# Ordering the casts of the middle features behind the weights' casts, and the loads for the weight sums behind other loads

## The chip, the core and the metric

One NeuronCore of a Trainium2 chip runs the whole layer as one program. The metric is the device time of one execution in microseconds (us). The kernel before takes 2896.6 us, the median of 3 runs (2887.7 to 2897.81).

## What is computed

The reference is one decoder layer on 2048 tokens of width 1024. The change touches its last line alone, the feed-forward part:

```python
h = rmsnorm(x, norm_mlp[l]) * (1.0 + sc_m) + sh_m
x = x + g_m * (jnp.square(jax.nn.relu(h @ w_ff1[l])) @ w_ff2[l])
```

`w_ff1` is 1024 x 4096 and `w_ff2` is 4096 x 1024, all in float32.

## The kernel before, in words

**Precision.** TensorE multiplies numbers of type float32r. Every float32 operand is therefore split into a high part, which is a cast to float32r on ScalarE, and a low part, which is the operand minus the high part. A product needs three matmuls: high by high, high by low, low by high. The weights' parts are `swh` and `swl` (function `left`, L1137 to L1144): the cast at L1142 on ScalarE, the subtraction at L1143 on VectorE in the first layer and on GpSimd in the second.

**Seven products for eight.** Both layers use a fast 2 x 2 block scheme: seven block products of sums of blocks, taken in the order `ORDER` = 0, 4, 5, 2, 6, 3, 1, instead of eight. The sums of `w_ff1` blocks (s4, s5, s2, s6) are made on GpSimd while the kernel runs (`lefts1`, L1146). The sums of `w_ff2` blocks are made once by `sums2` (L1233): it loads two tiles of 512 KB (L1238), makes four sums (L1239 and L1241 on GpSimd, L1240 and L1242 on VectorE) and stores two tiles to DRAM as `w2_d` (L1244).

**The loops.** The tokens are worked in two halves, `hf` = 1 and then 0. In each, the first layer runs 16 groups `g` of 256 middle features (`ff1`), seven products of 12 matmuls each, and stores the seven right-hand operands of each group to DRAM as `h_d` (256 KB each). In the first half only, each group also calls `sums2(g)`. Then the second layer (`ff2`) runs twice (`q` = 0, 1), 56 blocks each: 7 products by 8 groups. A block loads 256 KB of weights into `w` (L1323, 4 buffers, tag S), 256 KB of middle features into `bl` (L1325), casts them into `bh` (L1326, ScalarE), subtracts (L1327, VectorE), splits the weights (L1142, L1143) and does 12 matmuls (L1332 to L1334). `bh` and `bl` have 28 buffers each, `swh` and `swl` three. `load_y` fetches the tiles that the results are added to, and in the first half `load_h` prepares the next half's features; the scheduler places their instructions among those of the first layer's end and of `ff2`.

**What sets the order.** A scheduler writes each engine's instructions down in one fixed order when the kernel is built, and an engine works through its own list in that order. An instruction that waits holds up all behind it on that engine. Almost all loads and stores are issued by SyncE (SP), whose list is in order too. `tc.issue_after(x)` adds no semaphore; it makes the scheduler place what stands in the block behind `x` on the same engine. `gate["w1"]` is the latest load of `w_ff1` blocks (L1153).

Of the kernel before, what the change touches and what calls it, by code (L numbers as in the profile page):

```python
# [7 lines left out]
F32 = mybir.dt.float32  # L8
# [49 lines left out]
def tile_hybrid_layer(  # L58
# [17 lines left out]
    nc = tc.nc  # L76
    V, G, A, T = nc.vector, nc.gpsimd, nc.scalar, nc.tensor
# [56 lines left out]
    if True:  # L134
        def sb(name, bufs=1, stack=mx, side="left"):
            return stack.enter_context(tc.tile_pool(name=name, bufs=bufs, side=side))
# [9 lines left out]
        at = sb("at", 1, right, "right")  # L146
# [18 lines left out]
        gate = {"dma": None, "pe": None}  # L165
# [88 lines left out]
        def rstd(accs, which, name, pool=None, tag="mm"):  # L254


            v, r, t = [cp.tile([P, 4], F32, tag=n + which, name=n + name) for n in ("nv", "nr", "nt")]
            dg = accs[0]

            def sums():  # L260
                st = (pool or pm).tile([P, 4], F32, tag=tag, name="ss" + name)
                with tc.issue_after(gate["pe"]) if gate["pe"] is not None else nullcontext():
                    for b in range(4):
                        for i, acc in enumerate(accs):
                            T.matmul(st[:, b:b + 1], lhsT=acc[:, b * P:(b + 1) * P], rhs=ones[:, 0:1], start=i == 0,
                                     stop=i == len(accs) - 1)
                with tc.high_priority():
                  V.tensor_scalar(v, st, 1.0 / D, EPS, ALU.mult, ALU.add)
                  rsqrt(r, v, t)
                  for b in range(4):  # L270
                    V.tensor_scalar(dg[:, b * P:(b + 1) * P], ident, r[:, b:b + 1], None, ALU.mult)

            def spread():
                ps = (pool or pm).tile([P, CH], F32, tag=tag, name="rsp" + name)
                T.matmul(ps, lhsT=ones, rhs=dg, start=True, stop=True)
                A.copy(dg, ps)
            return sums, spread
# [748 lines left out]
        for k, tag in enumerate(("mt1", "mt0", "bv1", "bv0", "kw1", "kw0", "AT1", "AT0")):  # L1026
            x = dn.tile([P, CH], F32, tag=tag, name=f"x0_{k}")
# [56 lines left out]
        ORDER = (0, 4, 5, 2, 6, 3, 1)  # L1084
        fb = right.enter_context(tc.tile_pool(name="fb", bufs=28, side="right", reuse_waits="tile"))

        def right_tile(name):

            return [fb.tile([P, CH], F32R, tag=f"b{i}", name=f"b{i}{name}") for i in "hl"]
# [44 lines left out]

        def left(x, name, eng):  # L1137

            wh = wp.tile([P, CH], F32R, tag="wh", name="swh" + name)
            wl = wp.tile([P, CH], F32R, tag="wl", name="swl" + name)  # L1140
            with tc.high_priority():
                A.copy(wh, x)  # L1142
                eng.tensor_tensor(wl, x, wh.bitcast(F32), SUB)  # L1143
            return wh, wl  # L1144

        def lefts1(hf, g, unit):  # L1146

            nm = f"{hf}_{g}"
            a = []
            with tc.high_priority():  # L1150
                for i, t in enumerate(AB):
                    u = unit(t, f"{t}_1{nm}")
                    gate["w1"] = nc.sync.dma_start(u, w_ff1[g, i]).ins  # L1153
                    a.append(u)
                a11, a12, a21, a22 = a
                s4, s5, s2, s6 = [unit("S", f"s{i}{nm}") for i in (4, 5, 2, 6)]
                G.tensor_tensor(s4, a21, a22, ADD)
                G.tensor_tensor(s5, s4, a11, SUB)
                G.tensor_tensor(s2, a12, s5, SUB)
                G.tensor_tensor(s6, a11, a21, SUB)  # L1160
            xs = (a11, a12, s2, a22, s4, s5, s6)
            return lambda j: left(xs[j], f"{nm}_{j}", V)
# [27 lines left out]
        def unit(tag, name):  # L1190
            return fu.tile([P, CH], F32, tag=tag, name=name)
# [31 lines left out]
        def load_y(hf):  # L1223
            ys = []
            for k in range(KT):
                y = fy.tile([P, N2], F32, tag="y", name=f"y{hf}_{k}")
                for i in range(2):
                    with tc.issue_after(gate["w1"]):
                        nc.sync.dma_start(y[:, i * CH:(i + 1) * CH], x1_d[2 * hf + i][:, k, :])
                ys.append(y)  # L1230
            return ys

        def sums2(g):  # L1233

            y = [fy.tile([P, N2], F32, tag="y", name=f"ws2_{g}_{i}") for i in range(3)]
            (a11, a12), (a21, a22), (s4, s5) = [(t[:, 0:CH], t[:, CH:N2]) for t in y]
            for i in range(2):
                nc.sync.dma_start(y[i].rearrange("p (i c) -> p i c", i=2), w_ff2[g, 2 * i:2 * i + 2].rearrange("i p c -> p i c"))  # L1238
            G.tensor_tensor(s4, a21, a22, ADD)  # L1239
            V.tensor_tensor(s5, s4, a11, SUB)  # L1240
            G.tensor_tensor(a11, a11, a21, SUB)  # L1241
            V.tensor_tensor(a12, a12, s5, SUB)  # L1242
            for i in range(2):
                nc.sync.dma_start(w2_d[g][:, 2 * i:2 * i + 2], y[2 - 2 * i].rearrange("p (i c) -> p i c", i=2))  # L1244
# [56 lines left out]
            G.tensor_tensor(t4, t2, t21, SUB)  # L1301
            put(3, t4)

        def ff2(hf, q, ys):


            n1, n2 = 0, CH
            dst = {0: ((0, n1),), 1: ((0, n1),), 5: ((0, n2),), 2: ((0, n2),), 4: ((4, n2),), 6: ((4, n1), (4, n2)),
                   3: ((4, n1),)}
            chain = {0: "u", 5: "u", 6: "u", 4: "v", 2: "v", 3: "p", 1: "q"}  # L1310
            a, banks = q % 2, {}
            side = {"u": a, "v": 1 - a, "p": 1 - a, "q": a}
            final = {n: j for j in ORDER for n in dst[j]}
            for j in ORDER:
                ch = chain[j]
                start = ch not in banks
                if start:
                    banks[ch] = [pf.tile([P, CH], F32, tag=f"f{side[ch]}", name=f"f2{hf}_{q}_{j}{m}") for m in range(4)]
                for i in range(8):
                    g = 8 * q + i  # L1320
                    nm = f"2{hf}_{g}_{j}"
                    x, bt = unit("S", "w" + nm), right_tile(nm)
                    nc.sync.dma_start(x, {0: w_ff2[g, 0], 1: w_ff2[g, 1], 3: w_ff2[g, 3]}[j] if j in (0, 1, 3) else  # L1323
                                      w2_d[g][:, {4: 0, 5: 1, 6: 2, 2: 3}[j], :])
                    nc.sync.dma_start(bt[1].bitcast(F32), h_d[hf][g][:, j, :])  # L1325
                    A.copy(bt[0], bt[1].bitcast(F32))  # L1326
                    V.tensor_tensor(bt[1], bt[1].bitcast(F32), bt[0].bitcast(F32), SUB)  # L1327
                    wh, wl = left(x, nm, G)
                    for m in range(4):
                        s = slice(m * P, (m + 1) * P)  # L1330
                        ps = banks[ch][m]
                        T.matmul(ps, lhsT=wh[:, s], rhs=bt[0], start=start and i == 0, stop=False, skip_group_check=True)  # L1332
                        T.matmul(ps, lhsT=wh[:, s], rhs=bt[1], start=False, stop=False, skip_group_check=True)  # L1333
                        T.matmul(ps, lhsT=wl[:, s], rhs=bt[0], start=False, stop=i == 7, skip_group_check=True)  # L1334
                with tc.high_priority():
                    for m in range(4):
                        for m0, cs in dst[j]:
                            y = ys[m0 + m][:, cs:cs + CH]
                            gt = ngate[:, m0 + m:m0 + m + 1] if j == 3 else mods[:, 40 + m0 + m:41 + m0 + m]
                            V.scalar_tensor_tensor(y, banks[ch][m], gt, y, ALU.mult, ALU.add)  # L1340
                            if q == 1 and final[m0, cs] == j:
                                nc.sync.dma_start(yTv[:, m0 + m, hf * N2 + cs:hf * N2 + cs + CH], y)
# [6 lines left out]
        for hf in (1, 0):  # L1349
            if not hf:  # L1350
                get = lefts1(0, 0, unit)
            for g in range(NG):
                more = lefts1(hf, g + 1, unit) if g + 1 < NG else None
                if hf:
                    sums2(g)
                ff1(hf, g, bs, get)
                get = more
                if hf and g == 1:
                    for f in rstd([accs2[0]], "2", "20", pf, "f0"):
                        f()  # L1360
                if not hf and g == 4:
                    ys = load_y(0)
            if hf:
                ys = load_y(1)
            for q in range(2):
                ff2(hf, q, ys)
            if hf:
                bs = load_h(0, [accs2[0], accs2[1]])

# [87 lines left out]
```

## Time and profile before

| what | value |
|---|---|
| median of 3 runs | 2896.6 us |
| the profiled execution | 2896.35 us |
| its span, first to last instruction | 2894.6 us |
| TensorE busy (PE) | 2603.6 us, 90% |
| first layer, first half | 1537 to 1875 us of the span |
| second layer, first half | 1875 to 2242 us |
| first layer, second half | 2242 to 2547 us |
| second layer, second half | 2547 to 2891 us |

PE is TensorE's matmuls and PEld its weight loads, DVE is VectorE, ACT ScalarE, POOL GpSimd, SP SyncE. Matmuls are pipelined, so that a matmul's own time counts the one behind it too: read PE's speed by counting matmuls in a stretch, not by busy time. In a table of windows "(xN)" is the number of instructions that fall into the window, and PEclk is the share of the full TensorE clock that was granted.

### The profile page before, as it was taken

The page shows a single profiled execution, that of the slowest core. Times are in us where ns is not written, and L with a number is a line of the kernel's source. Part 1 is how long each engine was busy: PE and PEld are TensorE (multiplying, and loading weights), DVE is VectorE, ACT ScalarE, POOL GpSimd, SP SyncE. Part 2 cuts the span into 40 slices and gives each one's busy share as a digit, 9 for nine tenths or more (in the row PEclk, how much of TensorE's full clock was granted, in tenths as well). Part 3 has the DMA queues.
Part 4 walks back from the last instruction along what each step waited for, and adds up shares of the span by engine and source line. Part 5 has one row for each costly group of instructions (what it writes and reads, how often), then busy time and mean ns, then how long its engine had stood idle before and what let it go on. Part 6 is the DMA issues. An engine that isn't in the chain of part 4 may idle for free.

```text
span 2894.6 us, 40750 instructions
## 1 busy us (share of the span) xinstructions
PE 2603.6 (90%) x13684; PEld 2086.0 (72%) x13684; DVE 1575.3 (54%) x3359; ACT 1288.6 (45%) x2622; POOL 1049.7 (36%) x837
## 2 busy tenths in 40 slices
PE   4898799999989999888397999989999999999999
PEld 3687578877888688766275778866767888876667
DVE  7654886376437773375636664663335544473321
ACT  4553453346324553254432555653333555563331
POOL 3222201030103101131336786444448565553434
PEclk9999889999989999898698999999999999999999
DMA  8786677565556546352367974765544454485554
GB/s 306 267 286 208 225 270 250 169 209 168 179 171 201 184 155 215 122 183 82 100 201 268 319 255 148 271 236 160 168 152 146 155 206 149 147 282 161 167 156 135
DMA packets 327315, 566.86 MB, mean 196 GB/s; under 512 B 33512, under 2 KB 80552, under 8 KB 327080
## 3 DMA queue, kind: packets, MB, share of 16 engines
q1 hardware_dynamic: 308904, 534.63, 56.0%
q10 hardware_dynamic: 18176, 29.37, 2.8%
q8 instruction: 114, 1.87, 0.3%
q14 instruction: 121, 0.99, 0.1%
HBM read 403.86 MB, written 160.01 MB: 195 GB/s over the span
## 4 chain that ended last, share of the span: by engine, by line
PE 30%; issue 9%; POOL 9%; DMA 3%; DVE 2%; ACT 1%; POOLq 0%; SPq 0%; DVEq 0%; ACTq 0%
POOL swl L1143 6%; PE f L1257 6%; PE f L1259 6%; PE f L1258 6%; PE f L1334 3%; PE f L1333 3%; PE f L1332 3%; DMA bl<-h_d 1%; PE mmo L221 1%; PE mmo L222 1%; PE mmo L223 1%; DMA fx<-x_d 1%; POOL fx L1205 0%; POOL ws L1239 0%; DMA A<-in_w_ff_dram 0%
## 5 line engine op out<-in xcount | busy, mean ns | idle before, releaser
L1143 POOL TENSOR_TENSOR swl<-w,swh 128x512 fp32r<-128x512 f32 x224 | 304.8, 1363 | 379.5 <-ACT swh L1142 332.8
L1334 PE MATMUL f<-bh,swl 128*128 128x512 f32 x896 | 346.8, 405 | 32.8 <-POOL swl L1143 32.1
L1332 PE MATMUL f<-bh,swh 128*128 128x512 f32 x896 | 357.8, 399 | 19.5 <-ACT swh L1142 19.0
L1257 PE MATMUL f<-bh,swh 128*128 128x512 f32 x896 | 352.4, 393 | 16.3 <-ACT swh L1142 12.8
L1327 DVE TENSOR_TENSOR bl<-bl,bh 128x512 fp32r<-128x512 f32 x224 | 183.8, 836 | 333.8 <-ACT bh L1326 333.5
L1259 PE MATMUL f<-bh,swl 128*128 128x512 f32 x896 | 347.4, 393 | 12.6 <-DVE swl L1143 12.6
L1333 PE MATMUL f<-bl,swh 128*128 128x512 f32 x896 | 352.9, 394 | 0.0
L1258 PE MATMUL f<-bl,swh 128*128 128x512 f32 x896 | 351.1, 392 | 0.0
L1326 ACT CAST bh<-bl 128x512 fp32r<-128x512 f32 x224 | 136.8, 621 | 322.0 <-DMA bl<-h_d 287.2
L1334 PEld LDWEIGHTS f<-bh,swl 128*128 128x128 f32 x896 | 168.9, 189 | 107.7 <-POOL swl L1143 75.2
L1332 PEld LDWEIGHTS f<-bh,swh 128*128 128x128 f32 x896 | 169.9, 190 | 73.4 <-ACT swh L1142 38.3
L1257 PEld LDWEIGHTS f<-bh,swh 128*128 128x128 f32 x896 | 169.9, 190 | 54.9 <-ACT swh L1142 13.6
L1259 PEld LDWEIGHTS f<-bh,swl 128*128 128x128 f32 x896 | 169.5, 189 | 51.6 <-DVE swl L1143 16.4
L1258 PEld LDWEIGHTS f<-bl,swh 128*128 128x128 f32 x896 | 169.8, 189 | 35.2
L1333 PEld LDWEIGHTS f<-bl,swh 128*128 128x128 f32 x896 | 170.4, 190 | 30.7
L1143 DVE TENSOR_TENSOR swl<-s,swh 128x512 fp32r<-128x512 f32 x126 | 139.2, 1108 | 97.3 <-ACT swh L1142 97.0
L1142 ACT CAST swh<-w 128x512 fp32r<-128x512 f32 x224 | 138.2, 619 | 89.8 <-PE f L1333 67.0
L221 PE MATMUL mmo<-hm,who 128*128 128x512 f32 x256 | 103.4, 411 | 45.3 <-ACT hm L950 45.3
L932 POOL TENSOR_TENSOR o<-o,ro 128x512 f32<-128x512 f32 x16 | 16.7, 1042 | 323.7 <-DVE ro L129 159.3
L1143 DVE TENSOR_TENSOR swl<-A,swh 128x512 fp32r<-128x512 f32 x95 | 88.2, 928 | 77.3 <-ACT swh L1142 77.2
L1270 DVE TENSOR_TENSOR t<-t,f 128x512 f32<-128x512 f32 x128 | 87.1, 683 | 76.5 <-PE f L1259 73.3
L1271 ACT ACTIVATE t<-t 128x512 f32<-128x512 f32 x128 | 80.7, 630 | 86.6 <-DVE t L1270 86.6
(380 smaller groups left out, 6108.3 us busy)
## 6 DMA issues: line engine op xcount, KB each, us to landing
bl<-h_d SPq DMA_DIRECT2D x224, 256.0 KB
A<-in_w_ff_dram SPq DMA_DIRECT2D x128, 256.0 KB
h_d<-t SPq DMA_DIRECT2D x128, 256.0 KB
w<-w_d SPq DMA_DIRECT2D x128, 256.0 KB
wada<-in_w_ada_dram SPq DMA_DIRECT2D x48, 512.0 KB
h_d<-T SPq DMA_DIRECT2D x96, 256.0 KB
w<-in_w_ff_dram SPq DMA_DIRECT2D x96, 256.0 KB
wso<-in_w_out_dram SPq DMA_DIRECT2D x64, 256.0 KB
```

The costliest lines, as they stand in the source:

```text
L221: T.matmul(ps, lhsT=wh[:, k % 4, :], rhs=ah, start=k == 0, stop=False)
L1142: A.copy(wh, x)
L1143: eng.tensor_tensor(wl, x, wh.bitcast(F32), SUB)
L1257: T.matmul(ps, lhsT=wh[:, s], rhs=ah, start=start and k == 0, stop=False, skip_group_check=True)
L1258: T.matmul(ps, lhsT=wh[:, s], rhs=al, start=False, stop=False, skip_group_check=True)
L1259: T.matmul(ps, lhsT=wl[:, s], rhs=ah, start=False, stop=stop and k == 3, skip_group_check=True)
L1270: V.tensor_tensor(t, t, ps, op)
L1326: A.copy(bt[0], bt[1].bitcast(F32))
L1327: V.tensor_tensor(bt[1], bt[1].bitcast(F32), bt[0].bitcast(F32), SUB)
L1332: T.matmul(ps, lhsT=wh[:, s], rhs=bt[0], start=start and i == 0, stop=False, skip_group_check=True)
L1333: T.matmul(ps, lhsT=wh[:, s], rhs=bt[1], start=False, stop=False, skip_group_check=True)
L1334: T.matmul(ps, lhsT=wl[:, s], rhs=bt[0], start=False, stop=i == 7, skip_group_check=True)
```

## The change

Three edits. `left` now notes every weights' cast in a list, `casts`. The cast of the middle features of block `at` of a second layer is placed behind the weights' cast of block `at - 22` (for the first 25 blocks behind one of a nearer block, down to three casts before the layer begins). The two loads of `sums2` are placed behind the latest load of `w_ff1` blocks.

```diff
+        casts = []
+
         def left(x, name, eng):
...
             with tc.high_priority():
-                A.copy(wh, x)
+                casts.append(A.copy(wh, x).ins)
                 eng.tensor_tensor(wl, x, wh.bitcast(F32), SUB)
...
             for i in range(2):
-                nc.sync.dma_start(y[i].rearrange("p (i c) -> p i c", i=2), w_ff2[g, 2 * i:2 * i + 2].rearrange("i p c -> p i c"))
+                with tc.issue_after(gate["w1"]):
+                    nc.sync.dma_start(y[i].rearrange("p (i c) -> p i c", i=2), w_ff2[g, 2 * i:2 * i + 2].rearrange("i p c -> p i c"))
...
-        def ff2(hf, q, ys):
+        def ff2(hf, q, ys, base):
...
-            for j in ORDER:
+            for n, j in enumerate(ORDER):
...
-                    A.copy(bt[0], bt[1].bitcast(F32))
+                    at = 56 * q + 8 * n + i
+                    with tc.issue_after(casts[base + max(at - 22, at // 4 - 3)]):
+                        A.copy(bt[0], bt[1].bitcast(F32))
...
+            base = len(casts)
             for q in range(2):
-                ff2(hf, q, ys)
+                ff2(hf, q, ys, base)
```

The change adds and removes no instruction; it moves some. Three places follow. A name ends in the tile's numbers: `bh21_4_1` belongs to the second layer (2), half 1, group 4, product 1; `A11_11_0` is block A11 of the first layer's half 1, group 0.

ScalarE in the second layer, first half, `q` = 0, product 2 (blocks 28 to 31 are groups 4 to 7 of product 2), first before and then with the change. Product 1 is the last of the seven, so group 4 of it is block 52 and group 2 of it block 50.

```order
L1326 CAST bh21_4_1_32501<-bl21_4_1_32502 128x512
L1142 CAST swh21_4_2_31931<-w21_4_2_31924 128x512
L1326 CAST bh21_5_1_32524<-bl21_5_1_32525 128x512
L1142 CAST swh21_5_2_31954<-w21_5_2_31947 128x512
L1326 CAST bh21_6_1_32547<-bl21_6_1_32548 128x512
L1142 CAST swh21_6_2_31977<-w21_6_2_31970 128x512
```

```order
L1331 CAST bh21_2_1_32455<-bl21_2_1_32456 128x512
L1144 CAST swh21_5_2_31954<-w21_5_2_31947 128x512
L1331 CAST bh21_3_1_32478<-bl21_3_1_32479 128x512
L1144 CAST swh21_6_2_31977<-w21_6_2_31970 128x512
L1331 CAST bh21_4_1_32501<-bl21_4_1_32502 128x512
L1144 CAST swh21_7_2_32000<-w21_7_2_31993 128x512
```

Before, the features' cast of block 52 stands right ahead of the weights' cast of block 28, so 25 blocks ahead of the last weights' cast (27); with the change it stands behind the weights' cast of block 30, 22 ahead. SP's order of loads in this stage does not change: each weights' load of block m is followed by the features' load of block m + 22.

SP at the start of the first layer's first half, first before and then with the change; `fw_0` and the `A` tiles are blocks of `w_ff1`, `ws2` the loads of `sums2`, `w2_d` its stores.

```order
L1238 DMA ws2_0_0_28421<-in_w_ff2_dram 128x2x512
L1238 DMA ws2_0_1_28422<-in_w_ff2_dram 128x2x512
L1174 DMA fw_0_28349<-in_w_ff1_dram 128x512
L1238 DMA ws2_1_0_28586<-in_w_ff2_dram 128x2x512
L1238 DMA ws2_1_1_28587<-in_w_ff2_dram 128x2x512
L1244 DMA w2_d0_28333<-ws2_0_2_28423 128x1024
L1244 DMA w2_d0_28333<-ws2_0_0_28421 128x1024
L1238 DMA ws2_2_0_28790<-in_w_ff2_dram 128x2x512
L1153 DMA A11_11_0_28389<-in_w_ff1_dram 128x512
```

```order
L1176 DMA fw_0_28349<-in_w_ff1_dram 128x512
L1155 DMA A11_11_0_28389<-in_w_ff1_dram 128x512
L1155 DMA A11_11_1_28405<-in_w_ff1_dram 128x512
L1155 DMA A12_11_0_28391<-in_w_ff1_dram 128x512
L1155 DMA A12_11_1_28407<-in_w_ff1_dram 128x512
L1155 DMA A21_11_0_28393<-in_w_ff1_dram 128x512
L1155 DMA A21_11_1_28409<-in_w_ff1_dram 128x512
L1155 DMA A22_11_0_28395<-in_w_ff1_dram 128x512
L1155 DMA A22_11_1_28411<-in_w_ff1_dram 128x512
L1241 DMA ws2_0_0_28421<-in_w_ff2_dram 128x2x512
```

The nine loads of `w_ff1` blocks now go first. From there on one pair of `ws2` loads follows per group up to the last, where before all 16 pairs stood within the first seven groups.

POOL and DVE in the first layer's first half around groups 8 and 9, with the change; before, the same rows stand in the same order without the four of `ws2_9`.

```order
L1302 TENSOR_TENSOR T1_7_1_29823<-t1_7_3_29689,T1_7_0_29822 128x512
L1162 TENSOR_TENSOR s61_9_29847<-A11_11_9_29836,A21_11_9_29840 128x512
L1304 TENSOR_TENSOR T1_7_2_29824<-T1_7_1_29823,t1_7_2_29688 128x512
L1242 TENSOR_TENSOR ws2_9_2_30031<-ws2_9_1_30030 128x512
L1244 TENSOR_TENSOR ws2_9_0_30029<-ws2_9_0_30029,ws2_9_1_30030 128x512
L1159 TENSOR_TENSOR s41_10_30021<-A21_11_10_30017,A22_11_10_30019 128x512
```

```order
L1145 TENSOR_TENSOR swl1_9_0_30045<-A11_11_9_29836,swh1_9_0_30044 128x512
L1273 TENSOR_TENSOR t1_8_3_29866<-t1_8_3_29866,f11_8_0_29871 128x512
L1243 TENSOR_TENSOR ws2_9_2_30031<-ws2_9_2_30031,ws2_9_0_30029 128x512
L1273 TENSOR_TENSOR t1_8_2_29865<-t1_8_2_29865,f11_8_3_29963 128x512
L1245 TENSOR_TENSOR ws2_9_0_30029<-ws2_9_0_30029,ws2_9_2_30031 128x512
L1145 TENSOR_TENSOR swl1_9_4_30063<-s41_9_29844,swh1_9_4_30062 128x512
```

The low part for product 4 of group 9 now stands behind two sums of `sums2(9)` on DVE, and the sum s4 of group 10 behind two on POOL.

## Rows read from the trace of the kernel before

**Rows 1.** The page's first part: busy time, share, instructions of the engines.

```profile
PE 2603.6 (90%) x13684; PEld 2086.0 (72%) x13684; DVE 1575.3 (54%) x3359; ACT 1288.6 (45%) x2622; POOL 1049.7 (36%) x837
```

**Rows 2.** Windows, one per second layer: length, engines' busy time, PEclk, DMA share, GB/s.

```profile
1875.00:2242.00 367.00, 333.03 (x1348) 249.79 (x1348) 165.59 (x209) 150.51 (x262) 183.90 (x133) 0.98 0.55 177
2547.00:2891.00 344.00, 324.68 (x1346) 248.04 (x1344) 129.96 (x168) 122.91 (x216) 154.33 (x114) 1.00 0.53 171
```

**Rows 3.** Windows of L1334 alone (4 matmuls a block): PE, PEld, PEclk, DMA, GB/s.

```profile
1936.00:2173.00 237.00, 119.55 (x292) 54.82 (x291) 0.99 0.51 158
...
2604.00:2827.00 223.00, 113.00 (x276) 52.21 (x276) 0.99 0.51 161
2827.00:2889.00 62.00, 35.42 (x92) 17.15 (x92) 1.00 0.40 127
```

**Rows 4.** Windows of L1259 alone (first layer, 4 matmuls a product).

```profile
1537.00:1702.00 165.00, 79.00 (x196) 38.09 (x196) 0.95 0.88 313
...
1855.00:1875.00 20.00, 10.29 (x27) 5.07 (x27) 1.00 0.99 356
2242.00:2527.00 285.00, 160.56 (x419) 78.75 (x420) 1.00 0.46 161
```

**Rows 5.** Waits from 1936 to 2173: us in total, times, longest us.

```profile
ACT bh L1326 <- DMA bl<-h_d: 140.1, 67, 4.1
POOL swl L1143 <- ACT swh L1142: 109.8, 59, 4.0
...
PEld f L1334 <- POOL swl L1143: 33.8, 51, 1.4
```

**Rows 6.** Timelines of POOL, SP and ACT, 2041 to 2056: start, us, what [idle before].

```profile
2042.40 1.30 POOL L1143 TENSOR_TENSOR swl<-w,swh 128x512 fp32r<-128x512 f32 x1 [0.70 <-ACT swh L1142]
...
2043.73 0.33 SPq L1323 DMA_DIRECT2D w<-in_w_ff_dram  x1
2044.16 0.37 SPq L1325 DMA_DIRECT2D bl<-h_d  x1
...
2047.15 0.62 ACT L1326 CAST bh<-bl 128x512 fp32r<-128x512 f32 x1 [0.85 <-DMA bl<-h_d]
2047.67 0.62 ACT L1142 CAST swh<-w 128x512 fp32r<-128x512 f32 x1
...
2048.37 1.30 POOL L1143 TENSOR_TENSOR swl<-w,swh 128x512 fp32r<-128x512 f32 x1 [0.70 <-ACT swh L1142]
```

**Rows 7.** Timelines of SP, ACT and POOL where the first layer begins, 1529 to 1548.

```profile
1529.96 0.90 SPq L1238 DMA_DIRECT2D ws<-in_w_ff_dram  x2
1533.12 0.34 SPq L1174 DMA_DIRECT2D fw<-in_w_ff_dram  x1
...
1541.06 5.54 SPq L1153 DMA_DIRECT2D A<-in_w_ff_dram  x9
...
1536.69 1.14 ACT L1142 CAST swh<-fw 128x512 fp32r<-128x512 f32 x2 [4.94 <-DMA fw<-in_w_ff_dram]
...
1535.38 1.26 POOL L1239 TENSOR_TENSOR ws<-ws 128x512 f32<-128x512 f32 x1 [2.29 <-DMA ws<-in_w_ff_dram]
```

**Rows 8.** Timelines of POOL, SP and DVE in one group without sums, 1757 to 1780.

```profile
1758.20 1.30 POOL L1157 TENSOR_TENSOR s<-A,A 128x512 f32<-128x512 f32 x1 [5.92 <-DVE swl L1143]
...
1766.63 1.75 POOL L1299 TENSOR_TENSOR T<-t,T 128x512 f32<-128x512 f32 x1
...
1770.00 0.33 SPq L1153 DMA_DIRECT2D A<-in_w_ff_dram  x1
...
1776.47 0.69 DVE L1143 TENSOR_TENSOR swl<-s,swh 128x512 fp32r<-128x512 f32 x1
```

**Rows 9.** Groups of DVE from 1537 to 1702: xcount, busy us, mean ns, idle.

```profile
L1143 DVE TENSOR_TENSOR swl<-A,swh 128x512 fp32r<-128x512 f32 x21 | 25.3, 1204 | 8.2 <-ACT swh L1142 8.2
```

**Rows 10.** Windows of all engines where the second layer's first half begins.

```profile
1850.00:1860.00 10.00, 10.00 (x46) 8.29 (x45) 6.11 (x7) 6.20 (x12) 4.09 (x4) 1.00 0.50 146
1860.00:1900.00 40.00, 30.91 (x133) 24.28 (x131) 36.22 (x42) 29.54 (x54) 19.12 (x13) 0.94 1.05 401
```

## The prediction

> **What bounds the kernel now.** I read the page's busy times first, then windows over the four feed-forward stages, then the waits and timelines inside them. TensorE is busy for 90% of the span [rows 1], so only time in which TensorE is held up can be won. The windows of the two second layers [rows 2] show stages of 367 and 344 us in which no other engine is busy for more than half the time and DMA has a share of 0.55: nothing is full, so something waits in turn.
>
> How fast could TensorE go there? Count matmuls. In the first layer of the second half, 419 matmuls of L1259 stand in 285 us [rows 4]; four make a product of twelve, so a product takes 285 / 104.75 = 2.72 us, at a granted clock of 1.00. The end of the last second layer shows that its blocks of twelve can do the same: 92 matmuls of L1334, 23 blocks, in 62 us, 2.70 us each [rows 3]. From block 88 or so there are no features' casts left in ScalarE's list. Ahead of that, 73 blocks took 237 us in the first half and 69 blocks 223 us in the second [rows 3]. At 2.72 us they would have taken 198.6 and 187.7 us. **So 38.4 and 35.3 us are lost in the middle of the second layers, 73.7 us together.**
>
> The waits name the chain [rows 5]: ScalarE waits 140 us for the features' loads in its cast at L1326, GpSimd waits 110 us for ScalarE's weights' cast, and TensorE's weight loads wait for GpSimd's `swl`. The timeline shows that it closes into a ring [rows 6]. GpSimd ends a `swl` at 2043.70. That frees a weights' buffer; SP issues the load into it at 2043.73 and, only then, at 2044.16, the features' load that stands behind it. ScalarE gets this load for its cast at 2047.15, 3.0 us after the issue, makes the weights' cast behind it at 2047.67, and GpSimd's `swl` for that one begins at 2048.37. From `swl` to `swl` that is 5.97 us. By the lists it spans two blocks: the load of block m + 22 follows `swl` of block m - 4, and with a cast 25 ahead it stands before the weights' cast of block m - 2. Two blocks cost TensorE 5.44 us. The ring is slower, and a load that lands later than 3.0 us makes it slower still.
>
> **Part 1, the tie of the casts: -71 us.** With the cast 22 ahead, the load of block m + 22 is wanted only before the weights' cast of block m + 1. The ring then has five blocks, 13.6 us of TensorE's work, for the same 6 us. About 7 us of slack is more than any single wait of this chain in the rows (4.1 us). Nothing else is added: the same casts, 0.62 us each, two per block on ScalarE, 1.24 of 2.72 us. What is late next is the weights' own load: its ring is `swl` of block m - 4, load, cast, `swl` of block m, four blocks or 10.9 us for about 6 us. So the next limit is TensorE itself. Bounds: all 73.7 us, or 60 us if a fifth stays with waits of other kinds, such as the load of the next half's features among the last of these blocks. I take 71, close to the full amount, because the blocks without casts run at 2.70 us.
>
> **Part 2, the start of the first layer, first half: -3 us.** Before, SP issues two loads of sums, then `fw_0` at 1533.12, and ScalarE's first cast waits 4.94 us for it [rows 7]. With the change `fw_0` is issued where the sums' loads stood, 1529.96: 3.2 us earlier. Bounds 0 and 3.2.
>
> **Part 3, the first layer, first half, all groups: -21 us.** From 1537 to 1702 there are 196 matmuls of L1259, 49 products, worth 133.3 us [rows 4]; 31.7 us are lost, at a DMA rate of 313 GB/s. From 1855 to 1875 there are 27, 18.4 us, and 1.6 lost. Between them the layer loses nothing. So 33.3 us lie here. In the early groups all sums are crammed in, and the `A` loads come only at 1541.06, behind two pairs of loads and a store that waits for sums [rows 7]; with the change they follow `fw_0`. I leave 3 us for this start and 1.6 for the end.
>
> The sums do not vanish, though: every group gets one pair of loads, two sums on GpSimd and two on VectorE, and they make a new ring. GpSimd's s4 to the end of L1299 is five sums of 1.30 and one of 1.75, 8.25 us; from there (1768.38) SP reaches the place of the pair after the load at 1770.00 [rows 8] plus 0.33 and, for two issues, 0.90 [rows 7], 2.9 us; the pair lands; the sum at L1239 takes 1.26; VectorE then goes through two sums of `sums2`, one result and `swl` of product 4 at 0.69 each, 2.8 us; that `swl` frees the buffer for the next s4. The landing is bounded by two rows: 3.0 us for one load of a quarter of the pair's size [rows 6], and 4.5 us from the issue of the first pair (1530.86) to GpSimd's start (1535.38) [rows 7]; I estimate 4.0, between them, since the queue is less full later. Sum 19.2, with hand-overs about 19.5 us. A group costs TensorE 7 x 2.72 = 19.04. So the ring sits just above TensorE's pace: 16 x 0.46 = 7 us lost. 33.3 - 7 - 3 - 1.6 = 21.7, I take 21. Bounds: with 3.0 us the ring takes 18.5 and loses nothing, leaving -29; with 4.5 us and VectorE's 1.2 us per operation [rows 9] it takes 22.0, 47 us are lost where 33 were, and the part costs 18 us with the start's.
>
> The rows on VectorE speak against the change: `swl` takes 0.69 us with GpSimd idle [rows 8] and 1.20 on average while the sums run [rows 9]. The Trainium skill (SBUF — State Buffer, Who interferes with whom) says that a VectorE instruction with two SBUF inputs contends with a GpSimd instruction that reads SBUF, and that one then blocks fully until the other ends. By that rule the two engines' operations of a group would run one after the other, and the ring would be the upper one, 22.0 us. The trace has both durations, so I keep 0.69 where the ring's order itself makes GpSimd wait for VectorE, and the longer one as a bound.
>
> **Part 4, where the second layer's first half begins: +5 us.** From 1860 to 1900 DMA runs at 401 GB/s, share 1.05, and TensorE already loses time there, while from 1850 to 1860 the share is 0.50 [rows 10]. The last two groups' sums now come right before: 4 MB, 10 us at that rate, of which half fits the slack. Hidden entirely it costs 0, not hidden at all 10 us. The load of the next half's features still stands among these blocks, so the old loss there stays. In the second half the same place has no sums.
>
> **Sum.** -71 - 3 - 21 + 5 = -90 us. The profiled execution took 2896.35 us (span 2894.6), which is the median of the runs, 2896.6, within 0.3 us. 2896.35 - 90 = **2806 us**. The first layer of the second half and all before 1530 stay as they are.
>
> **Rivals.**
> - *The sums' ring paces the first layer.* It needs the upper durations of part 3. For it: VectorE's 1.20 us while GpSimd is busy. Against it: the sums were twice as dense there. 2896.35 - 71 - 3 + 18 + 5 = 2845 at its worst, 2838 with a ring of 21.5 us. By the rule of the Trainium skill in part 3 it would be the first of these.
> - *The next wait takes over in the second layer.* The weights' load lands late too, or ScalarE's own list holds up, and half the loss remains: 2896.35 - 36 - 3 - 21 + 5 = 2841. Against it: four blocks of slack, and in the rows it is the features' load that ScalarE waits for.
> - *Slower.* GpSimd stands in its list at L1239 until the pair lands, with s4 of the next group behind it. If DMA is as full as at 1860 to 1900 throughout, and the pair lands late, the ring grows one for one. It decides once it eats all gains: 33.3 - 4.6 + 3 + 71 - 5 = 98 us over 16 groups is 6.1 us, a ring of 25.2 us and a landing of 9.7 us. A landing of 12 us would give a ring of 27.5 us, 135 us lost, and 2934 us. Against it: no row has a landing above 4.5 us.
> - *The tie changes nothing.* The lists do move, so this asks that a load landing 7 us earlier be no help: 2896.35 - 3 - 21 + 5 = 2877 by parts 2 to 4 alone.
>
> **Chances.** Forecast 0.74, its own range 2790 to 2832; the sums' ring 0.13; half the loss 0.06; slower 0.03; no effect of the tie 0.04. The lower end is all bounds on the good side: 73.7 + 3.2 + 29 + 0 = 106, 2790, and some of the old loss at the start of the second layer, 4 us. The upper end takes in the sums' ring and half the loss, 2845. About 0.5%, 14.5 us, is what a measurement of this kernel can tell from no change: faster than 2882 has 0.94, within it 0.03, slower 0.03.
>
> **What would show it.** Right: 112 blocks of a second layer in about 305 us plus its start; ScalarE's wait for the features' load gone from hundreds of us to a few; weight loads of L1334 no longer waiting for `swl`; first layer's groups of 19 to 20 us from the second on. Wrong: ScalarE still waits in the features' cast (L1331 in the changed kernel) for `h_d` (the ring was not the cause); or it waits for `w` in its place; or GpSimd waits at the first of its sums (L1242 there) for the sums' loads and groups take 21 us or more; or the second layer's first half begins with a longer stall than before.

## The result: faster by 1.1%, 55 us short of the forecast

| | before | changed kernel | forecast |
|---|---|---|---|
| median time | 2896.55 us (4 runs) | 2861.61 us (4 runs, 2856.55 to 2870.91) | 2806 (2786 to 2845) |
| ratio | 1 | 0.989, interval 0.9857 to 0.9922 | 0.969 |
| profiled execution, span | 2896.35, 2894.6 | 2859.91, 2858.1 | |

The kernel became faster, by 35 us where 90 were forecast, and the time lies above the range. The profiled executions differ by 36.4 us. From the first matmul of each feed-forward stage to that of the next (the last stage: to its last block), the two traces split it like this, in us:

| stage | before | changed | difference |
|---|---|---|---|
| up to the first layer | 1537.4 | 1538.2 | +0.8 |
| first layer, first half | 337.9 | 369.8 | **+31.9** |
| second layer, first half | 366.4 | 331.8 | **-34.6** |
| first layer, second half | 305.5 | 305.6 | +0.1 |
| second layer, second half | 342.0 | 307.3 | **-34.7** |

The differences add up to -36.5. So both second layers gave what was forecast, and nearly half of it was lost again in the first layer's first half, where a gain was forecast.

### The profile after: the second layers

The page's first part and two groups of its fifth part (xcount | busy us, mean ns | idle before) in the changed kernel:

```profile
PE 2579.9 (90%) x13684; PEld 2105.0 (74%) x13684; DVE 1651.4 (58%) x3359; ACT 1286.4 (45%) x2622; POOL 1041.4 (36%) x837
...
L1332 DVE TENSOR_TENSOR bl<-bl,bh 128x512 fp32r<-128x512 f32 x224 | 263.8, 1194 | 159.0 <-ACT bh L1331 158.8
L1331 ACT CAST bh<-bl 128x512 fp32r<-128x512 f32 x224 | 135.2, 615 | 2.2 <-DMA bl<-h_d 2.2
```

The group of the features' casts in the kernel before:

```profile
L1326 ACT CAST bh<-bl 128x512 fp32r<-128x512 f32 x224 | 136.8, 621 | 322.0 <-DMA bl<-h_d 287.2
```

Busy times tell little, as in [rows 1]. The windows of the last matmul line alone (L1339 in the changed kernel; four matmuls a block) answer to [rows 3]:

```profile
1972.00:2160.00 188.00, 107.58 (x277) 51.86 (x277) 1.00 0.64 194
2590.00:2827.00 237.00, 135.47 (x349) 65.50 (x349) 1.00 0.60 184
```

277 matmuls are 69.25 blocks in 188 us, and 349 are 87.25 blocks in 237 us: 2.71 and 2.72 us a block, where [rows 3] had 3.25 and 3.23. The waits of the first of these stretches answer to [rows 5] (us in total, times, longest us):

```profile
ACT swh L1144 <- POOL swl L1145: 109.0, 69, 1.6
POOL swl L1145 <- ACT swh L1144: 99.6, 70, 1.4
DVE bl L1332 <- ACT bh L1331: 69.5, 52, 1.4
DVE y L1345 <- PE f L1339: 10.1, 8, 1.3
```

ScalarE's wait for the features' load is gone, from 287.2 us to 2.2 on the page, and in no row is it TensorE that waits. ScalarE and GpSimd still wait for one another 100 us each, and it costs nothing: they run at TensorE's pace and idle the rest of each block. VectorE's subtraction became longer, 1194 ns on average against 836 in the kernel before, at no cost either.

### The profile after: the first layer, first half

Windows of L1262 alone, answering to [rows 4]:

```profile
1564.00:1890.00 326.00, 159.89 (x394) 77.60 (x394) 0.94 0.65 227
1890.00:1908.00 18.00, 10.15 (x27) 4.96 (x27) 1.00 1.02 374
2240.00:2525.00 285.00, 160.55 (x419) 78.64 (x420) 1.00 0.47 161
```

394 matmuls are 98.5 products in 326 us, 3.31 us each, against 2.72 in the two windows below it. A group takes 23.2 us on average (groups 1 to 14, from 20.2 to 26.1 us); before, from group 8 on, it took 19.0. The granted clock averages 0.94 in the first window; in the turn shown below nothing waits for TensorE. The waits of the first window:

```profile
ACT t L1274 <- DVE t L1273: 101.6, 55, 9.3
POOL ws L1242 <- DMA ws<-in_w_ff_dram: 79.0, 13, 7.7
DVE ws L1243 <- POOL ws L1242: 70.6, 14, 7.2
...
PE f L1262 <- DVE swl L1145: 32.8, 13, 4.2
POOL s L1159 <- DVE swl L1145: 16.6, 13, 1.8
```

Read it from the second row. GpSimd stands 6 us in each group at the first sum of `sums2` until the pair of loads lands. VectorE waits for that sum, TensorE for VectorE's `swl`, and GpSimd's next s4 for the buffer that this `swl` frees. That is the ring of part 3. Timelines of GpSimd, SP and VectorE around one turn of it (start, us, idle before and what ended it):

```profile
1752.09 1.29 POOL L1159 TENSOR_TENSOR s<-A,A 128x512 f32<-128x512 f32 x1 [1.23 <-DVE swl L1145]
1754.07 1.28 POOL L1160 TENSOR_TENSOR s<-s,A 128x512 f32<-128x512 f32 x1 [0.68 <-POOL s L1159]
1755.31 1.73 POOL L1298 TENSOR_TENSOR T<-t,t 128x512 f32<-128x512 f32 x1
1757.00 1.73 POOL L1161 TENSOR_TENSOR s<-A,s 128x512 f32<-128x512 f32 x1
...
1759.95 1.74 POOL L1302 TENSOR_TENSOR T<-t,T 128x512 f32<-128x512 f32 x1
1761.65 1.29 POOL L1162 TENSOR_TENSOR s<-A,A 128x512 f32<-128x512 f32 x1
1762.90 1.74 POOL L1304 TENSOR_TENSOR T<-T,t 128x512 f32<-128x512 f32 x1
1771.16 1.29 POOL L1242 TENSOR_TENSOR ws<-ws 128x512 f32<-128x512 f32 x1 [6.52 <-DMA ws<-in_w_ff_dram]
1773.26 1.26 POOL L1244 TENSOR_TENSOR ws<-ws,ws 128x512 f32<-128x512 f32 x1 [0.81 <-DVE ws L1243]
1775.75 1.29 POOL L1159 TENSOR_TENSOR s<-A,A 128x512 f32<-128x512 f32 x1 [1.23 <-DVE swl L1145]
```

```profile
1762.62 0.38 SPq L1155 DMA_DIRECT2D A<-in_w_ff_dram  x1
1763.05 1.06 SPq L1241 DMA_DIRECT2D ws<-in_w_ff_dram  x2
```

```profile
1772.49 0.69 DVE L1243 TENSOR_TENSOR ws<-ws,ws 128x512 f32<-128x512 f32 x1 [5.89 <-POOL ws L1242]
1773.10 0.68 DVE L1273 TENSOR_TENSOR t<-t,f 128x512 f32<-128x512 f32 x1
1773.69 1.38 DVE L1245 TENSOR_TENSOR ws<-ws,ws 128x512 f32<-128x512 f32 x1
1774.99 0.68 DVE L1145 TENSOR_TENSOR swl<-s,swh 128x512 fp32r<-128x512 f32 x1
```

From s4 to s4 that is 23.66 us, by the terms of part 3:

| term | predicted | traced |
|---|---|---|
| GpSimd, s4 to the end of L1302 | 8.25 | 9.60 |
| SP, until both loads are issued | 2.9 | 2.42 |
| landing of the pair | **4.0** | **7.05** |
| first sum, to VectorE's start | 1.26 | 1.33 |
| VectorE, four operations | 2.8 | 3.18 |
| hand-over | 0.3 | 0.08 |
| sum | 19.5 | 23.66 |

The landing is the largest error, 3.05 of the 4.15 us. It varies: counted in the same way it took 5.6 to 7.5 us in the eleven turns that begin from 1589 to 1823, with a median of 6.75. All engines in a window of those microseconds, in the changed kernel:

```profile
1765.00:1770.00 5.00, 5.00 (x24) 4.14 (x23) 1.29 (x2) 2.43 (x5) 0.00 (x0) 1.00 0.96 297
```

The DMA engines are at a share of 0.96 while GpSimd does nothing. In the kernel before, in a group without sums, the share was 0.27 from 1765 to 1770 and 0.43 from 1757 to 1780. SP issues the pair right behind `A` loads and among the stores of products: from 1761.71 to 1765.48 three `A` loads, two stores and the pair, 2.4 MB together. At 297 GB/s that is about 8 us, an estimate.

### The profile page after: what moved, and what is told of

It is laid out like the page before. It is cut to its first block, busy times and chain, and to the rows that moved or that the text cites. A ratio compares the mean times of both kernels' runs of the same rounds, so it can differ in the third digit from the quotient of the medians.

```text
span 2858.1 us, 40676 instructions
## 1 busy us (share of the span) xinstructions
PE 2579.9 (90%) x13684; PEld 2105.0 (74%) x13684; DVE 1651.4 (58%) x3359; ACT 1286.4 (45%) x2622; POOL 1041.4 (36%) x837
## 5 line engine op out<-in xcount | busy, mean ns | idle before, releaser
L1262 PE MATMUL f<-bh,swl 128*128 128x512 f32 x896 | 353.5, 400 | 33.2 <-DVE swl L1145 33.2
L1337 PE MATMUL f<-bh,swh 128*128 128x512 f32 x896 | 352.0, 393 | 13.3 <-ACT swh L1144 13.3
L1332 DVE TENSOR_TENSOR bl<-bl,bh 128x512 fp32r<-128x512 f32 x224 | 263.8, 1194 | 159.0 <-ACT bh L1331 158.8
L1339 PE MATMUL f<-bh,swl 128*128 128x512 f32 x896 | 335.4, 392 | 7.7 <-POOL swl L1145 7.7
L1262 PEld LDWEIGHTS f<-bh,swl 128*128 128x128 f32 x896 | 172.5, 193 | 75.8 <-DVE swl L1145 39.1
L1339 PEld LDWEIGHTS f<-bh,swl 128*128 128x128 f32 x896 | 169.5, 190 | 45.1 <-POOL swl L1145 9.8
L1261 PEld LDWEIGHTS f<-bl,swh 128*128 128x128 f32 x896 | 173.1, 193 | 36.6 <-issue 0.2
L932 POOL TENSOR_TENSOR o<-o,ro 128x512 f32<-128x512 f32 x16 | 16.6, 1040 | 320.4 <-DVE ro L129 158.3
```

The lines of the kernel that those rows point to most:

```text
L1261: T.matmul(ps, lhsT=wh[:, s], rhs=al, start=False, stop=False, skip_group_check=True)
L1262: T.matmul(ps, lhsT=wl[:, s], rhs=ah, start=False, stop=stop and k == 3, skip_group_check=True)
```

## The experiments

The theory after this reading: the two edits act apart; the tie of casts is worth some 70 us, and the tie of loads makes the sums' ring pace the first layer, mostly through the landing. All ratios are to the kernel before.

### The two edits apart

The tied casts alone (the loads of `sums2` free):

```diff
             for i in range(2):
-                with tc.issue_after(gate["w1"]):
-                    nc.sync.dma_start(y[i]..., w_ff2[g, 2 * i:2 * i + 2]...)
+                nc.sync.dma_start(y[i]..., w_ff2[g, 2 * i:2 * i + 2]...)
```

> The tie of the casts alone, the sums' loads free as before. If the two edits act apart, the second layers gain the 35 and 36 us that the changed kernel shows there and the first layer's first half stays at its 338 us of before: about 2896 - 71 = 2825 us. Rival: the sums spread out are what lets the second layer run at 2.72 us a block (less DMA and GpSimd work left over at its start); then the blocks stay above 2.72 us and the time is above 2850 us.

Measured: 2822.12 us, ratio 0.9756 (0.9732 to 0.9779). The first layer's first half takes 338.4 us (before 337.9), the second layers 324.7 and 308.4.

The tied loads alone:

```diff
-                    with tc.issue_after(casts[base + max(at - 22, at // 4 - 3)]):
-                        A.copy(bt[0], bt[1].bitcast(F32))
+                    A.copy(bt[0], bt[1].bitcast(F32))
```

> The tie of the sums' loads alone, the features' casts free as before. If the edits act apart: first layer's first half 33 us longer, groups of 23 to 24 us, second layers as before: about 2896 + 33 = 2930 us. Rival: the longer first layer is a consequence of the moved casts; then about 2897 us.

Measured: 2930.36 us, ratio 1.0133 (1.0111 to 1.0155). The first layer's first half takes 371.3 us. Waits in it, 1560 to 1850, and in the second layer behind it, 1980 to 2210:

```profile
POOL ws L1242 <- DMA ws<-in_w_ff_dram: 73.1, 12, 7.6
```

```profile
ACT bh L1330 <- DMA bl<-h_d: 138.6, 66, 3.5
```

Both as expected. **The second edit alone makes the kernel slower by 1.3%**, the first alone faster by 2.4%, and 0.9756 x 1.0133 = 0.9886 is the changed kernel's ratio. Each wait belongs to one edit: the one for the sums' loads comes with the second, the one for the features' loads stays unless the first is there.

### A cast 24 blocks ahead

```diff
-                    with tc.issue_after(casts[base + max(at - 22, at // 4 - 3)]):
+                    with tc.issue_after(casts[base + max(at - 24, at // 4 - 3)]):
```

Made in the version with the tied casts alone.

> The tie of the casts alone, with 24 blocks for 22 (the scheduler's own list has 25). Ring theory: at 25 the ring has two blocks (5.4 us of TensorE's work for 6 us), at 24 three (8.2 us), at 22 five: a step, so 2820 to 2830 us as with 22. Rival: each block of distance gives a share (fewer buffers in flight, less crowding), so that 24 keeps two thirds of the loss: about 2865 us.

Measured: 2820.35 us, ratio 0.9745 (0.9714 to 0.9777), the same as at 22. Three blocks in the ring are as good as five: 25 ahead, the scheduler's own order (no tie at 25 was run), lost half a microsecond a block, at 24 every block of the middle takes 2.72 us. So it is a step, and not a share for each block of distance.

### What makes the ring long

The load that GpSimd's first sum wants is issued first (in `sums2`):

```diff
-            for i in range(2):
+            for i in (1, 0):
```

> Both ties, but the pair's second load, which GpSimd's first sum reads, goes first. Ring theory (landing, GpSimd's sum, VectorE's sums, swl of product 4, s4, the sums of GpSimd, the next pair): GpSimd's first sum then runs while the other load lands, and the ring of 23.7 us loses about 1.3 us a group, 15 to 20 us in all: 2842 to 2847 us. Rival, crowding (VectorE and GpSimd slow each other, so that the work of a group takes 23.7 us wherever it stands): the same time, 2862 us.

Measured: 2859.61 us, ratio 0.9901 (0.9868 to 0.9934). A miss. GpSimd's wait fell as expected, from 79.0 to 61.6 us in 13 waits, 1.3 us each, but the first layer's first half only from 369.8 to 365.3 us. The other load, which VectorE wants, now came last: VectorE's first sum waited 19.3 us for a load in 4 waits, where it had waited for none. Both loads are needed within 2 us of one another, so their order is worth little. The time is the rival's, so this run alone does not decide between the two.

Half the bytes:

```diff
-                    nc.sync.dma_start(y[i]..., w_ff2[g, 2 * i:2 * i + 2]...)
-            G.tensor_tensor(s4, a21, a22, ADD)
+                    nc.sync.dma_start(y[i][:, 0:CH], w_ff2[g, 2 * i])
+            G.tensor_tensor(s4, a21, a21, ADD)
...
-            V.tensor_tensor(a12, a12, s5, SUB)
+            V.tensor_tensor(a12, s4, s5, SUB)
```

> The changed kernel with one thing smaller: the two loads of sums2 bring 256 KB each instead of 512 KB, and the four sums, of the same shape and on the same engines, read only what was brought (half of each pair of weight blocks is left out of the computation). Theory, the landing of the pair sets the pace of the first layer's first half: in the changed kernel it lands 7.05 us after its issue in a stretch of 297 GB/s; 0.5 MB less is 1.8 us less at that rate, and VectorE's list has one result more between GpSimd's sum and product 4 (0.7 us). So GpSimd's wait for the loads falls from about 6.1 to about 4.3 us a group, and the first half's first layer from 368 to 340-352 us (13 to 16 groups by 1.1 to 1.8 us), the time from 2862 to 2834-2846 us. Rival, the slower operations of GpSimd and VectorE beside one another set the 23.7 us: their number is the same, so the groups stay and the time is 2857 us or more (with 0.7 us a group longer, up to 2873). Second rival, what holds the pair back is its place behind the other transfers and not its size: the landing stays near 7 us and the time near 2862 us.

This kernel leaves out half of each pair of weight blocks, so it is of use for its times alone. Measured: 2843.95 us, ratio 0.9838 (0.9814 to 0.9861). Its first layer's first half takes 354.1 us, 15.7 less (from the first to the last matmul of L1262, as the expectation counts, 352.0 for 367.7). Timelines of SP and GpSimd, and the waits from 1560 to 1890, in this version:

```profile
1752.27 1.02 SPq L1241 DMA_DIRECT2D ws<-in_w_ff_dram  x2
```

```profile
1741.26 1.29 POOL L1159 TENSOR_TENSOR s<-A,A 128x512 f32<-128x512 f32 x1 [1.82 <-DVE swl L1145]
...
1749.17 1.74 POOL L1302 TENSOR_TENSOR T<-t,T 128x512 f32<-128x512 f32 x1
...
1758.35 1.04 POOL L1242 TENSOR_TENSOR ws<-ws 128x512 f32<-128x512 f32 x1 [4.48 <-DMA ws<-in_w_ff_dram]
...
1763.30 1.30 POOL L1159 TENSOR_TENSOR s<-A,A 128x512 f32<-128x512 f32 x1 [1.83 <-DVE swl L1145]
```

```profile
POOL ws L1242 <- DMA ws<-in_w_ff_dram: 56.8, 14, 5.1
```

The pair lands 5.06 us after its issue, 2.0 us sooner, and the turn shrinks from 23.66 to 22.04 us, less by the landing's 2.0 but for one more result in VectorE's list. GpSimd's and VectorE's operations are the same in number and shape. In the eleven turns the landing takes 4.6 to 5.7 us, with a median of 5.0 for 6.75. So the landing sets the pace, and about 2 of its 7 us are half of the pair's own bytes. How the other 5 divide between the other half and the transfers around it is not shown.

### Opening the ring

First the sums of a group are made one group after their loads, behind s6 on GpSimd (`load2` is the two loads of `sums2`, which keeps the rest):

```diff
-                G.tensor_tensor(s6, a11, a21, SUB)
+                gate["s6"] = G.tensor_tensor(s6, a11, a21, SUB).ins
...
+            with tc.issue_after(gate["s6"]):
+                G.tensor_tensor(s4, a21, a22, ADD)
...
-                    sums2(g)
+                    load2(g)
+                    if g:
+                        sums2(g - 1)
```

> Both ties, and the sums of a pair are made one group after its loads (behind s6 of the next group but one on GpSimd), so that the landing falls out of the ring; the same operations on the same engines. Ring theory: groups of 19.0 to 19.6 us from the second on instead of 23.7, the first layer's first half 310 to 318 us instead of 368, 2805 to 2820 us in all. Rival, crowding: groups still above 22 us, 2840 us or more.

Measured: 2849.3 us, ratio 0.9867 (0.9838 to 0.9896); first layer, first half, 360.0 us. A miss: time and groups (22.3 us on average) are those of the rival. Yet GpSimd no longer waits for the sums' loads; a new row stands in its place (waits, 1560 to 1850):

```profile
POOL s L1159 <- DMA A<-in_w_ff_dram: 90.1, 12, 8.8
```

s4 wants blocks A21 and A22. The A21 load of the next group stood on SP behind the stores of `w2_d`, and these waited for VectorE's sums: SP's list closes a second ring of nearly the same length. So, on top of this edit, the loads of the pair go behind the A21 load, and the stores (`put2`) one group later still:

```diff
+                    if i == 2:
+                        gate["a21"] = gate["w1"]
...
-                with tc.issue_after(gate["w1"]):
+                with tc.issue_after(gate["a21"]):
...
+                    if g > 1:
+                        put2(g - 2)
```

> As the run with the sums a group later, and SP's list changed so that nothing of the sums stands ahead of a load of w_ff1 blocks: the pair's loads behind the load of A21, the stores of the sums one group later again. In the run before this one GpSimd's wait had moved from the pair's landing to A21's, which stood on SP behind the pair and behind stores that wait for VectorE. Ring theory: now no landing is left in the ring, groups of 19.0 to 19.6 us, first layer's first half 308 to 318 us, 2800 to 2815 us in all. Rival, crowding on VectorE and GpSimd or in the DMA queue: groups stay above 21 us, 2835 us or more.

Measured: 2827.8 us, ratio 0.9767 (0.9739 to 0.9795); first layer, first half, **330.8 us against 369.8**. Waits from 1560 to 1850:

```profile
POOL s L1161 <- DVE swl L1145: 58.7, 14, 4.4
DVE ws L1253 <- POOL ws L1252: 47.8, 13, 3.7
...
POOL s L1162 <- DMA ws<-in_w_ff_dram: 10.9, 11, 1.0
```

From the fourth to the fourteenth the groups run at a steady 19.9 to 20.0 us, 0.9 over TensorE's own 19.0, with the same loads, sums and stores. So the rival, crowding, falls. The time missed its expectation by 13 us: the groups were expected at 19.0 to 19.6, and the second layer's first half, which now begins with a longer stall, takes 335.9 us, 4 more than in the changed kernel.

This run also weighs the rule of the Trainium skill (SBUF — State Buffer, Who interferes with whom), by which a VectorE instruction with two SBUF inputs and a GpSimd instruction that reads SBUF contend, and the later one is blocked until the other ends. The trace agrees. In the changed kernel's turn above, VectorE's L1245 starts at 1773.69, while GpSimd's L1244 runs. It takes 1.38 us, where such an operation alone takes 0.69, and ends 0.55 us after GpSimd's. In that kernel's whole first layer, first half, 97 such VectorE operations start during one of GpSimd's (more than 0.2 us before its end); all of them end 0.54 to 0.56 us after it. Likewise 64 of GpSimd's start during one of VectorE's, and all end 1.12 to 1.16 us after it.

In the turn above this lengthens two of GpSimd's six operations from s4 to the end of L1302 against [rows 8], by 0.43 us each, and one of VectorE's four, by 0.69. (The rest of GpSimd's 9.60 for 8.25 is idle time, 0.68 us before L1160.) That is at most 1.6 us of the ring's excess of 4.15, and with the ring open all of a group's operations still fit into 19.9 us. So the blocking is real here, but it alone would not have set 23.7.

### The start of the second layer

The next half's features (`load_x`) are loaded and scaled among the first blocks of the second layer. Here they are spread over blocks 12 to 57, with the ring open:

```diff
+            with behind("sp"):
+                nc.sync.dma_start(x, x1_d[2 * hf + n][:, kk, :])
+            with behind("dve"):
+                V.tensor_tensor(x, x, rs[n], ALU.mult)
+            with behind("act"):
+                A.activation(x, x, AF.Identity, scale=..., bias=...)
```

> As the kernel with the ring open, and the loads of the next half's features, VectorE's and ScalarE's work on them spread over blocks 12 to 57 of the second layer's first half, where they stood among blocks 4 to 12. If these operations, waiting in ScalarE's and VectorE's lists for a full DMA queue, make the stall of 17 to 19 us at that place, it shrinks to under 5 us and the time is 12 to 17 us below the kernel with the ring open. Rival: the stall comes from the features' own loads of the second layer's first 24 blocks; then the same time.

Measured: 2809.62 us, ratio 0.9723 (0.9689 to 0.9756), 18 below the version before it. The second layer's first half goes from 335.9 to 323.3 us, 12.6 of the 18; 6 more stand ahead of the feed-forward part, which nothing in the edit touches (the first layer starts at 1535.1 and not at 1541.1), and are not put down to it. The stall does not shrink to under 5 us, though: the first 16 blocks go from 66.4 to 54.6 us, and at 2.72 us each they would take 43.5. The same in the version with the tied casts alone:

> The tied casts alone, without the tied loads of the sums, and with them the loads and sums for the next half's middle features spread over blocks 12 to 57 of the second layer instead of its first blocks. If the stall at the start of the second layer's first half is that work standing before the first casts and products, it falls here as it did beside the opened ring: 12 to 18 us less than the tied casts alone (2822), about 2804 to 2810 us. Rival: without the tied loads the stall there has another cause, and the time stays at 2822 us.

Measured: 2813.34 us, ratio 0.9711 (0.9689 to 0.9732). The mechanism holds and the size is smaller: 324.7 to 315.9 us, 8.8. There the stall at the start was smaller to begin with: the first 16 blocks took 56.0 us, and 66.4 with the ring open.

Last, VectorE's two sums placed behind its `swl` of product 1, with the ring open and the features later (the second sum likewise):

```diff
+            with tc.issue_after(lows[V]):
+                V.tensor_tensor(s5, s4, a11, SUB)
```

> The version with the features later, and in it VectorE's two sums of a group are moved behind its last result of product 1, so that VectorE no longer stands before GpSimd's first sum. If the 0.9 us a group that the first layer's first half still loses at product 1 is VectorE waiting for that sum (47.8 us in 13 waits in the version with the ring open), the groups go from 19.9 to 19.0-19.3 us and the time from 2810 to about 2798 us (2795 to 2803). Rival: GpSimd's round of sums and small features itself, not VectorE's place in it, sets 19.9; then the groups stay and the time is about 2810 us.

Measured: 2805.22 us, ratio 0.9692 (0.9667 to 0.9718), the fastest of all, though its interval overlaps that of the version before it. It lies between the expectation (2795 to 2803) and its rival (2810). The groups went only from 19.9 to 19.7 us: the first layer's first half is 4.9 us shorter, and the second layer's first half 4.2 longer, than in that version. Waits from 1560 to 1850:

```profile
DVE ws L1261 <- POOL ws L1259: 16.6, 13, 2.4
PEld f L1285 <- ACT t L1294: 13.5, 14, 3.2
```

VectorE's wait for GpSimd fell from 47.8 to 16.6 us. TensorE now waits for ScalarE's copies of products (L1294, t<-f). What holds them back, and so the 0.7 us a group that remain, stays open: no run takes VectorE's wait for GpSimd away altogether.

## Why the prediction was right and wrong

**Part 1, the tie of the casts: right.** -71 was predicted. The second layers became 34.6 + 34.7 = 69.3 us shorter, and that is after 2.1 us more of stall at the first half's start, so -71.4. The tied casts alone give 75.3, 3.9 of it at that start, which is 71.4 again. The ring of two blocks was the cause: with three or five blocks in it every block of the middle runs at TensorE's pace, and the wait for `h_d` is gone. The one turn that was read, 5.97 us, was a short one: it explains half of the loss, and from 1940 to 2170 the mean from one `swl` to the next but one is 6.49 us, which explains all of it (3.25 us a block). The forecast did not suffer, since it counted the loss from the blocks. The rivals "the next wait takes over" and "no effect" fall.

**Part 2, the earlier start: nothing came of it.** The step that failed took the place in SP's list for the time of the issue. The first load of `w_ff1` waits for GpSimd's last accumulation of the part before (L966), and it did so in the kernel before too. Timelines of GpSimd, before and with the change, and of SP with the change (before: [rows 7]):

```profile
1531.83 1.26 POOL L966 TENSOR_TENSOR acc<-acc,nq 128x512 f32<-128x512 f32 x1 [4.15 <-ACT nq L965]
```

```profile
1533.68 1.26 POOL L966 TENSOR_TENSOR acc<-acc,nq 128x512 f32<-128x512 f32 x1 [4.14 <-ACT nq L965]
```

```profile
1534.97 0.33 SPq L1176 DMA_DIRECT2D fw<-in_w_ff_dram  x1
1535.39 6.97 SPq L1155 DMA_DIRECT2D A<-in_w_ff_dram  x8
```

That operation ends at 1533.09 before and at 1534.94 with the change, and the load is issued 0.03 us later in both. Removing the sums' loads ahead of it took nothing off that wait. The +0.8 us by itself would show little: the first layer begins between 1531.4 and 1544.2 us in the twelve traces.

**Part 3, the first layer's first half: wrong, and it is the whole miss.** -21 was predicted, +31.9 came: 53 of the 53.5 us by which the sum of the stages misses -90. The ring was drawn rightly, link by link, and two of its terms were mis-sized. The larger is the landing: "I estimate 4.0, between them, since the queue is less full later". It took 7.05. Both rows used for it were of other circumstances: one load of 256 KB, and a pair issued alone. The bound of 4.5 was no bound, since neither row had the `A` loads and stores of a whole group in flight with it. The other is GpSimd's stretch from s4 to the end of L1299: "8.25 us" adds up six durations and leaves out the idle time between them. The two lines of [rows 8] at its ends, 1758.20 and 1766.63 with 1.75, are already 10.18 us apart; with the change it took 9.60. With 10.18 the sum would have come to 21.4 us a group, and part 3 to a cost of some 10 us in place of a gain of 21. VectorE's 3.18 for 2.8 is small, and SP's 2.42 for 2.9 makes up for it. With 23.2 us a group, fourteen groups lose 14 x (23.2 - 19.04) = 58 us where the forecast had 7.

The first rival named this outcome, "the sums' ring paces the first layer", with 22.0 us as its worst and a chance of 0.13. The right row to watch stood at the end of the forecast: GpSimd waits at the first of its sums and groups take 21 us or more. The "slower" rival's mechanism was this one too; with the landing at 7.05 of its 9.7 us it ate half of the gain.

**Part 4, the start of the second layer's first half: the size right, the net by two effects.** The first 16 blocks take 62.0 us where they took 59.9: +2.1 for +5. The runs with one edit each take it apart: 64.7 us with the tied loads alone, +4.8, and 56.0 with the tied casts alone, -3.9; from there to both ties it is +6.0. So the sums right ahead cost about what was forecast, and the tied casts won some 4 us there that the prediction did not have. All engines in the first 40 us of this stage, before and with the change:

```profile
1875.00:1915.00 40.00, 28.36 (x104) 21.49 (x104) 35.65 (x43) 28.21 (x50) 18.68 (x11) 0.84 0.88 334
```

```profile
1908.00:1948.00 40.00, 26.44 (x100) 20.10 (x99) 36.12 (x42) 25.74 (x46) 16.59 (x11) 0.87 0.93 349
```

DMA is a little fuller than before, 0.93 for 0.88, and VectorE is busy for 36 of the 40 us in both; that the cost comes by way of DMA, as the prediction had it, is not shown. The runs with the features later show that part of that stall is the next half's features, standing ahead of the first blocks' work: the first 16 blocks fall to 54.6 us with the ring open, and to 47.2 with the tied casts alone. At 2.72 us they would take 43.5; what holds up the rest stays open.

**Sum.** Predicted -71 - 3 - 21 + 5 = -90. Traced: -71.4, +0.8, +31.9 and +2.1, which gives -36.6.

## What to carry to other kernels

A load that is issued "just in time" next to the load it is tied to also lands together with it: price its landing by the bytes in flight at that moment (here 7.05 us), not by a lone load in a quiet row (3.0 us). A stretch of an engine's list is as long as from its first start to its last end, idle time included, and not the sum of its durations. When work is moved from a crammed place to an even pace, follow its links round; if the consumer stands in the same in-order list as the producer of the next turn, the even pace becomes a ring, and the whole landing is paid once per turn. A lookahead that closed an in-order ring within two blocks lost time on every block; one block fewer was enough to win it all back.

## What was not expected of the hardware

- A pair of 512 KB loads took 7.05 us to land with the DMA engines at a share of 0.96 and 297 GB/s, and 5.06 us at half the size in the same place. The mean rate of the whole stretch was 227 GB/s: the mean share of 0.65 hides the bunch.
- In the second layers VectorE's subtraction went from 836 to 1194 ns on average, and no block became longer for it. In the new order it starts while GpSimd's `swl` runs, and ends 0.55 us after it, as in these lines of the changed kernel. From 65 to 260 us into the second layer's first half 69 of 71 do so; in the kernel before, 2 of 61.

```profile
2069.32 1.30 POOL L1145 TENSOR_TENSOR swl<-w,swh 128x512 fp32r<-128x512 f32 x1 [1.42 <-ACT swh L1144]
...
2069.80 1.37 DVE L1332 TENSOR_TENSOR bl<-bl,bh 128x512 fp32r<-128x512 f32 x1 [1.35 <-ACT bh L1331]
```
